# S5 octet steps of a hybrid decoder block at later places in the program: products and maps, the first states, all outputs

## The chip, the core and the metric

The kernel runs on one core of a Trainium2 chip. The metric is device time in microseconds, the median of the timed executions: 818.08 us for the kernel before (three runs, 817.52 to 818.77). The profile is that of one more execution, which took 814.82 us.

## The reference

One layer of a decoder trunk, width 2048, 512 tokens, batch 1. A normalised input goes through one wide projection, whose columns feed three head groups: an S5 branch (a diagonal complex state space model), differential attention, and cross-attention into 256 memory tokens. What they give is gated, put side by side, projected once more, normalised and added to the input.

```python
h = rmsnorm(x, g_pre)
cols = h @ w_in        # S5 u | S5 gate | diff q, k, v, gate | mem q, gate
...
# S5 branch: 64 groups of 16 channels, 64 complex states each
bu = einsum('tgh,gph->tgp', u, bbar)            # bbar, abar from dt, a, b
x_t = abar * x_{t-1} + bu_t                     # scan over the 512 tokens
y = Re(einsum('tgp,ghp->tgh', x, c)) + d * u    # then GELU, GLU, SiLU gate
...
out = x + rmsnorm(concat(heads) @ w_out, g_post)
```

## The kernel before

**The stream of chunks.** Every big matrix product is a list of chunks; one chunk is a piece of a weight matrix of 128x1024 values (512 KB). The chunks are worked off one after the other in the loop at the end of the kernel (from `for n, (_, f) in enumerate(chunks)`). For each, SyncE issues a DMA into `raw` (two buffers); ScalarE casts it to `whi` (three buffers), which holds the high part of the values; VectorE subtracts to get `wlo`, the rest; TensorE then does 24 matmuls of 128x512 in groups of three (`mm3`: high by high, low by high, high by low). The names `hhi`, `hlo` are the two parts of the normalised input. A load is issued two or three chunks ahead of its use, a cast one or two.

**The slots.** Each chunk is cut into four units of six matmuls. After each unit the loop calls what `at_slot(n, f)` has entered for that quarter of chunk n; `round(4 * n) + 3` is the number of the unit. So the table of slots (lines 716 to 744) says between which units a step stands in the program. TensorE keeps the program's order (`pin`). On VectorE, ScalarE and SyncE the scheduler that lays out the program orders the instructions, and each engine works its row off in that order.

**Stages.** Chunks 0 to 15 make u, the input of the S5 branch (eight column blocks of two chunks). Chunks 16 to 23 and 24 to 31 make the keys and values of the memory (the first of these with matmuls of 256 columns on `mhi`, `mlo`, the two parts of the memory tokens; a small step of TensorE on `diag`, the tokens' scales, stands soon after octet 3's weights). From chunk SG = 32 on come the S5 gate and further columns; from S1 = 64 on the GLU of the S5 branch.

**The S5 steps.** The 64 groups are handled as eight octets. For each octet there are, early:

- products (line 540), in two halves: VectorE makes `bp` and the first part of `dp` in the first half, `pm` and the rest of `dp` in the second. A DMA fetches `bc`, another writes `dp` to `sp_dr` in DRAM.
- maps (line 566): four transposes of `bp` by TensorE, a copy by ScalarE, a DMA to `sp_dr`.
- weights (line 573): 16 small matmuls of `dp` and `bp` by TensorE, then copies into `kz` and a DMA to `k_dr`.

And late, from chunk 33 on, one octet per 3.25 chunks:

- load (line 606): a DMA brings `sp_dr` back as `sp` (two buffers), the last reader of which is the octet's outputs.
- angles (line 632): GpSimd and VectorE make `cs`, ScalarE turns it into sine and cosine (three ACTIVATE rows on `cs`).
- spread (line 646): ScalarE copies `sp` into the two tiles `ub` (four copies).
- states (line 652), in six parts: 16 matmuls of `us` and `ub` by TensorE into two banks of `ps_s`; then VectorE's work: products with `cs` (`ra`), sums (`wre`, `wim`), eight scans (`zre`, `zim`), products again, and four writes to `x` (two per half).
- outputs (line 689): eight matmuls of `us` and `tm` and 16 of `x` and `sp` by TensorE into `ps_t`; then a GELU by ScalarE (square, tanh) and VectorE (`sq`, `ysb`); after each second octet DMAs to `y_dr`. `ge_open` reads it back for the GLU.

VectorE besides has `ut` and `ev` (evacuations of a finished column block), `mlo` (the low part of the memory tokens) and `wlo`. ScalarE has one table of functions at a time: between tanh and sine stands an ACT_TABLE_LOAD.

Lines 71, 96 and 99 of the profile are helpers: 71 is the line through which most instructions of the other engines are recorded, 96 a matmul, 99 a transpose. So groups and rows are told apart by the names of their tiles.

Of the kernel before, what the change touches and what calls it, by code (L numbers as in the profile page):

```python
# [54 lines left out]
def tile_hybrid_block(ctx: ExitStack, tc: tile.TileContext, a: dict, out: bass.AP):  # L55
# [33 lines left out]
    def psum(tag):  # L89
        return ps.tile([P, 512], F32, tag=tag, name=f"ps_{tag}", bufs={"mm": 4, "s": 2, "t": 2}[tag])  # L90
# [4 lines left out]
    def mm(*args, **kw):  # L95
        pin(pe.matmul(*args, **kw))  # L96
# [98 lines left out]
    def at_slot(n, f):  # L195
        side.setdefault(round(4 * n) + 3, []).append(f)
# [343 lines left out]
    def s5_products(o):  # L540


        bc = pt("bc", [512], 2)
        sy.dma_start(bc, a["bc"][o])
        gr = slice(8 * o, 8 * o + 8)

        def powers(t_, n):
            return t_[:, gr, :].unsqueeze(3).to_broadcast([P, 8, n, 16])

        def params(i, n):  # L550
            return bc[:, i * P:(i + 1) * P].rearrange("p (g h) -> p g h", g=8).unsqueeze(2).to_broadcast([P, 8, n, 16])

        bp, dp = pre["bp", o], pre["dp", o] = pt("bp", [8, LCH, 16]), pt("dp", [8, LCH + 1, 16], 2)
        m2 = pt("pm", [8, LCH + 1, 16])
        v.tensor_tensor(bp, powers(w1, LCH), params(0, LCH), ALU.mult)
        v.tensor_tensor(m2[:, :, 0:LCH], powers(w2, LCH), params(1, LCH), ALU.mult)
        v.tensor_tensor(bp, bp, m2[:, :, 0:LCH], ALU.add)
        v.tensor_tensor(dp, powers(pwr, LCH + 1), params(2, LCH + 1), ALU.mult)
        yield
        m2 = pt("pm", [8, LCH + 1, 16])  # L560
        v.tensor_tensor(m2, powers(npwi, LCH + 1), params(3, LCH + 1), ALU.mult)
        v.tensor_tensor(dp, dp, m2, ALU.add)
        sy.dma_start(sp_dr[o][:, 0:640], dp.rearrange("p g j h -> p (g j h)"))
        yield

    def s5_maps(o):
        pp_, up = psum("t"), pt("up", [512])
        for q in range(4):
            transpose(pp_[:, q * P:(q + 1) * P], pre["bp", o][:, 2 * q:2 * q + 2].rearrange("p x b h -> p (x b h)"))
        s.copy(up, pp_)  # L570
        sy.dma_start(sp_dr[o][:, 640:1152], up)
# [29 lines left out]
    oct_ = [{} for _ in range(8)]  # L601

    def t512(tag, bufs=1, shape=(P, 512)):
        return s5["wk"].tile(list(shape), F32, tag=tag, name=tag, bufs=bufs)

    def s5_load(o):

        sp = t512("sp", 2, (P, 1152))
        sy.dma_start(sp, sp_dr[o])
        oct_[o].update(dp=sp[:, 0:640].rearrange("p (g j h) -> p g j h", g=8, h=16), up=sp[:, 640:1152])  # L610
# [13 lines left out]
    def s5_toeplitz(i, x):  # L624

        tm = s5["d"][i % 2]["tm"]
        kd = k_dr[i].rearrange("(x q r) e -> x r q e", x=2, r=32)
        for b_ in range(LCH):
            r0 = 64 * x + 16 * b_
            sy.dma_start(tm[r0:r0 + 16, :, x * 64:(x + 1) * 64], kd[x, 0:16, :, 16 * b_:16 * b_ + 64])  # L630
# [15 lines left out]
    def s5_spread(o):  # L646
        for i in range(2):
            for x in range(2):
                rows = slice(64 * x, 64 * x + 64)
                s.copy(s5["ub"][i][rows, :, x], oct_[o]["up"][rows].rearrange("p (q i m) -> p q i m", q=4, i=2)[:, :, i])  # L650

    def s5_states(o):

        x, ub, us, (c_, s_) = s5["d"][o % 2]["x"], s5["ub"], oct_[o]["us"], oct_[o]["cs"]
        vre, vim = psum("s"), psum("s")
        for q in range(4):
            sl = slice(q * P, (q + 1) * P)
            mm(vre[:, sl], ub[0][:, q].rearrange("p x m -> p (x m)"), us[:, q], start=True, stop=True)
            mm(vim[:, sl], ub[1][:, q].rearrange("p x m -> p (x m)"), us[:, q], start=True, stop=True)
        yield  # L660
        a1, a2, a3, a4 = t512("ra", 2), t512("ra", 2), t512("ra", 2), t512("ra", 2)
        wre, wim = t512("wre"), t512("wim")
        v.tensor_tensor(a1, vre, c_, ALU.mult)
        v.tensor_tensor(a2, vim, s_, ALU.mult)
        v.tensor_tensor(wre, a1, a2, ALU.add)
        yield
        v.tensor_tensor(a3, vim, c_, ALU.mult)
        v.tensor_tensor(a4, vre, s_, ALU.mult)
        v.tensor_tensor(wim, a3, a4, ALU.subtract)
        yield  # L670
        zre, zim = t512("zre"), t512("zim")
        for q in range(4):
            sl = slice(q * P, (q + 1) * P)
            rbc = rch[:, 4 * o + q:4 * o + q + 1].to_broadcast([P, P])
            v.tensor_tensor_scan(zre[:, sl], rbc, wre[:, sl], 0.0, ALU.mult, ALU.add)
            v.tensor_tensor_scan(zim[:, sl], rbc, wim[:, sl], 0.0, ALU.mult, ALU.add)
        yield
        xg = x.rearrange("p (q x) c -> p q x c", x=2)
        for i, (y1, y2, op) in enumerate(((zre, zim, ALU.subtract), (zim, zre, ALU.add))):
            b1, b2 = t512("ra", 2), t512("ra", 2)  # L680
            v.tensor_tensor(b1, y1, c_, ALU.mult)
            v.tensor_tensor(b2, y2, s_, ALU.mult)
            for g_ in range(2):
                rows = slice(64 * g_, 64 * g_ + 64)
                b1_, b2_ = (t_[rows].rearrange("p (q c) -> p q c", q=4) for t_ in (b1, b2))
                v.tensor_tensor(xg[64 * i:64 * i + 64, :, g_, 1:], b1_, b2_, op)
            yield

    def s5_outputs(o):

        d, us = s5["d"][o % 2], oct_[o]["us"]
        yp = psum("t")
        cols_ = [slice(q * P, (q + 1) * P) for q in range(4)]
        for q in range(4):
            mm(yp[:, cols_[q]], s5["d"][o // 2 % 2]["tm"][:, 4 * (o % 2) + q], us[:, q], start=q == 0, stop=False,
               skip_group_check=True)
        for q in range(4):
            for x in range(2):
                mm(yp[64 * x:64 * x + 64, cols_[q]], oct_[o]["dp"][:, 2 * q + x, 1:].rearrange("p j h -> p (j h)"),
                   d["x"][:, 2 * q + x, 0:NCH], start=False, stop=True, tile_position=(0, 64 * x), skip_group_check=True)  # L700
        if o % 2 == 0:
            s5["y"] = t512("ysb", 2, (P, 2, 512))
        ysb = s5["y"]
        sq = t512("sq")
        s.activation(sq, yp, AF.Square)
        v.scalar_tensor_tensor(sq, sq, 1.0 / GELU_A, yp, ALU.add, ALU.mult)
        s.activation(sq, sq, AF.Tanh, scale=GELU_A * GELU_S)
        v.scalar_tensor_tensor(ysb[:, o % 2], sq, 1.0, yp, ALU.add, ALU.mult)
        if o % 2 == 1:
            dst = y_dr[o // 2].rearrange("(q x h) (j c) -> j x h q c", x=2, h=16, j=LCH)  # L710
            for x in range(2):
                for j in range(LCH):
                    r0 = 64 * x + 16 * j
                    sy.dma_start(dst[j, x], ysb[r0:r0 + 16].rearrange("p o (q c) -> p (o q) c", c=NCH))

    SG = S0 + 16
    STEPS = (0, 0.25, 0.75, 1, 1.5, 2)
# [1 line left out]
    at_slot(8, pre_open)  # L719
    at_slot(8, discretise)  # L720
    for o in range(8):
        e = 8.75 + 1.75 * o if o < 4 else 17.5 + 3.25 * (o - 4)
        d = 2 if o < 4 else 4
        at_slot(e, lambda o=o: (oct_[o].setdefault("pr", s5_products(o)), next(oct_[o]["pr"])))
        at_slot(e + d / 2, lambda o=o: next(oct_[o]["pr"]))
        at_slot(e + 0.75 * d, lambda o=o: s5_maps(o))
        at_slot(e + (2 if o < 4 else 3), lambda o=o: s5_weights(o))
# [3 lines left out]
    for o in range(8):  # L731
        e = SG + 1 + 3.25 * o
        at_slot(e - 0.75, lambda o=o: s5_angles(o))
        at_slot(e - 0.5, lambda o=o: s5_spread(o))
        for i in range(6):
            at_slot(e + STEPS[i] + (0 if o else 0.25), lambda o=o, i=i: (oct_[o].setdefault("st", s5_states(o)), next(oct_[o]["st"])))
        if o > 1:
            at_slot(e - 3, lambda o=o: s5_load(o))
            if o % 2 == 0:
                for x in range(2):  # L740
                    at_slot(e - 3.25 + 0.75 * x, lambda o=o, x=x: s5_u(o // 2, x))
                    at_slot(e - 4.5 + 0.75 * x, lambda o=o, x=x: s5_toeplitz(o // 2, x))
        at_slot(e + 3.25, lambda o=o: s5_outputs(o))
    S5_END = SG + 1 + 3.25 * 7 + 4.5


# [123 lines left out]
    for h in range(4):  # L870
        e = S2 + 2 + 3 * h
# [99 lines left out]
    for h in range(4):  # L971
        add_cols(a["w_in_a"], [20 + h], h_cols, NK, lambda i, acc, h=h: evac_k(h, acc))
        add_cols(a["w_in_a"], [16 + h], h_cols, NK, lambda i, acc, h=h: evac_q(h, acc))
        for qt in range(NT):
            e = S3 + 5 + 4 * h + (qt if h < 3 else qt // 2)
# [222 lines left out]
```

## Time and profile before

| | |
|---|---|
| timed runs, median | 818.08 us (817.52 to 818.77) |
| the profiled execution | 814.82 us |
| its span | 813.0 us |
| GpSimd (POOL) busy | 27.7 us |
| HBM traffic | 161 GB/s over the span |

A row of the timeline gives start, duration, engine, line, operation, tiles and count; in brackets stands how long the engine was idle before it and what ended that. A row of the table of waits gives the tile that the waiting instruction writes, the engine and tile waited for, then microseconds in all, how many times, and the longest. Matmul durations overlap their successors, so the pace is read from starts.

### The profile page before, as it was taken

How to read it: one execution, taken by the hardware profiler on the slowest of the kernel's cores; microseconds unless marked ns; L12 is line 12 of the kernel's file. 1: busy time of each engine (PE TensorE's matmuls, PEld its weight loads, DVE VectorE, ACT ScalarE, POOL GpSimd, SP SyncE). 2: the span in 40 equal slices, each digit the busy share in tenths (PEclk: the TensorE clock that was granted, in tenths of full speed). 3: DMA queues.
4: the chain of work that ended last, by engine and by line, in shares of the span. 5: the costliest groups of instructions: out<-in, count | busy, mean ns of one | idle time of the engine just before them, and what ended most of it. 6: DMA issues, size and time to landing. Idle time of an engine off the chain costs nothing.

```text
span 813.0 us, 10918 instructions
## 1 busy us (share of the span) xinstructions
PE 792.1 (97%) x4030; PEld 661.2 (81%) x4030; DVE 545.2 (67%) x1033; ACT 357.8 (44%) x593; POOL 27.7 (3%) x42
## 2 busy tenths in 40 slices
PE   8998999999999899999999999999999999999996
PEld 7876798778888787888888888888888888888885
DVE  4599978578887898847875544668888833132335
ACT  5654433433546344334733533446667532132311
POOL 0000000200000000000000000000100110000000
PEclk9999999999999999999999999999999999999999
DMA  7977767766445464367565222232224345322327
GB/s 262 369 271 248 259 218 250 251 176 190 134 151 174 112 165 116 120 171 260 185 209 168 93 92 91 78 104 78 79 77 145 96 155 174 104 86 96 114 95 258
DMA packets 60358, 131.59 MB, mean 162 GB/s; under 512 B 12689, under 2 KB 26129, under 8 KB 59409
## 3 DMA queue, kind: packets, MB, share of 16 engines
q1 hardware_dynamic: 60304, 130.91, 49.8%
q8 instruction: 31, 0.51, 0.3%
q14 instruction: 23, 0.18, 0.1%
HBM read 109.52 MB, written 21.36 MB: 161 GB/s over the span
## 4 chain that ended last, share of the span: by engine, by line
PE 73%; DVE 13%; DMA 5%; ACT 4%; issue 4%; SPq 1%; DVEq 0%; POOLq 0%; POOL 0%; ACTq 0%
PE ps_mm L96 65%; PE ps_s L96 4%; DVE wlo L71 3%; DVE ra L71 3%; DMA raw<-in_w_in_a_dram 2%; PE ps_t L96 2%; ACT whi L71 2%; PE ps_t L99 1%; DVE x L71 1%; DMA raw<-in_w_kv_b_dram 1%; ACT cs L71 1%; DMA sp<-sp_dr 1%; SPq L71 1%; DVE zim L71 1%; ACT L71 1%
## 5 line engine op out<-in xcount | busy, mean ns | idle before, releaser
L71 DVE TENSOR_TENSOR wlo<-raw,whi 128x1024 fp32r<-128x1024 f32 (+1 forms) x135 | 161.7, 1199 | 155.4 <-ACT whi L71 154.4
L71 ACT CAST whi<-raw 128x1024 fp32r<-128x1024 f32 (+1 forms) x135 | 138.7, 1029 | 258.4 <-PE ps_mm L96 144.0
L96 PE MATMUL ps_mm<-hhi,whi 128*128 128x512 f32 x512 | 201.5, 394 | 1.1 <-DVE ut L71 0.7
L96 PE MATMUL ps_mm<-hlo,whi 128*128 128x512 f32 x512 | 199.9, 390 | 0.7 <-DVE hlo L71 0.7
L96 PE MATMUL ps_mm<-hhi,wlo 128*128 128x512 f32 x512 | 199.6, 390 | 0.0
L96 PEld LDWEIGHTS ps_mm<-hhi,whi 128*128 128x128 f32 x512 | 96.2, 188 | 21.6 <-DVE ut L71 1.1
L96 PEld LDWEIGHTS ps_mm<-hhi,wlo 128*128 128x128 f32 x512 | 96.1, 188 | 20.6
L96 PEld LDWEIGHTS ps_mm<-hlo,whi 128*128 128x128 f32 x512 | 96.2, 188 | 20.5 <-DVE hlo L71 1.6
L96 PE MATMUL ps_mm<-whi,hhi 128*128 128x512 f32 x128 | 50.0, 390 | 0.0
L96 PE MATMUL ps_mm<-whi,hlo 128*128 128x512 f32 x128 | 49.9, 390 | 0.0
L96 PE MATMUL ps_mm<-wlo,hhi 128*128 128x512 f32 x128 | 49.9, 389 | 0.0
L96 PE MATMUL ps_mm<-whi,yshi 128*128 128x512 f32 (+1 forms) x112 | 43.9, 392 | 0.0
L96 PE MATMUL ps_mm<-wlo,yshi 128*128 128x512 f32 (+1 forms) x112 | 43.3, 387 | 0.0
L96 PE MATMUL ps_mm<-whi,yslo 128*128 128x512 f32 (+1 forms) x112 | 43.3, 386 | 0.0
L96 PEld LDWEIGHTS ps_mm<-whi,hlo 128*128 128x128 f32 x128 | 24.0, 188 | 5.1
L96 PEld LDWEIGHTS ps_mm<-wlo,hhi 128*128 128x128 f32 x128 | 24.0, 188 | 4.8
L96 PEld LDWEIGHTS ps_mm<-whi,hhi 128*128 128x128 f32 x128 | 24.0, 188 | 4.7
L71 DVE TENSOR_TENSOR x<-ra 64x512 f32<-64x512 f32 x32 | 26.3, 821 | 0.8
L71 ACT ACTIVATE pr<-sm,nm 128x128 f32<-128x128 f32 (+3 forms) x32 | 18.0, 564 | 18.9 <-DVE nm L71 18.6
L96 PE MATMUL ps_mm<-gehi,whi 128*128 128x512 f32 x64 | 25.2, 394 | 0.0
L96 PE MATMUL ps_mm<-gehi,wlo 128*128 128x512 f32 x64 | 25.1, 392 | 0.0
L96 PE MATMUL ps_mm<-whi,yxhi 128*128 128x512 f32 (+1 forms) x64 | 24.9, 389 | 0.0
(323 smaller groups left out, 1381.6 us busy)
## 6 DMA issues: line engine op xcount, KB each, us to landing
raw<-in_w_in_a_dram SPq DMA_DIRECT2D x63, 512.0 KB, 4.0
raw<-in_w_out_b_dram SPq DMA_DIRECT2D x32, 512.0 KB, 3.2
raw<-in_w_in_b_dram SPq DMA_DIRECT2D x16, 512.0 KB, 3.3
sp<-sp_dr SPq DMA_DIRECT2D x8, 576.0 KB, 4.5
rows<-in_x_dram SPq DMA_DIRECT2D x4, 1024.0 KB, 7.7
raw<-in_w_kv_a_dram SPq DMA_DIRECT2D x8, 512.0 KB, 3.6
raw<-in_w_kv_b_dram SPq DMA_DIRECT2D x8, 512.0 KB, 4.0
raw<-in_w_glu_a_dram SPq DMA_DIRECT2D x8, 512.0 KB, 5.1
```

What stands on the lines that cost most here:

```text
L71: r = f(*args, **kw)
L96: pin(pe.matmul(*args, **kw))
L99: pin(pe.transpose(o, i, ident))
```

## The change

Four numbers in the table of slots change. Products (both halves), maps and weights of octets 0 to 3 move by 0.75 chunk: from slots 8.75, 10.5, 12.25, 14 to 9.5, 11.25, 13, 14.75; those of octets 4 to 7 stay. The six parts of the states of octet 0 move by 0.25 chunk. The outputs of every octet move by 0.5 chunk, and with them the load of `sp` for octets 2 to 7. Slots that are not named stay, S5_END too. No instruction of the steps themselves is added or removed.

```diff
     for o in range(8):
-        e = 8.75 + 1.75 * o if o < 4 else 17.5 + 3.25 * (o - 4)
+        e = 9.5 + 1.75 * o if o < 4 else 17.5 + 3.25 * (o - 4)
         d = 2 if o < 4 else 4
...
         for i in range(6):
-            at_slot(e + STEPS[i] + (0 if o else 0.25), lambda o=o, i=i: (oct_[o].setdefault("st", s5_states(o)), next(oct_[o]["st"])))
+            at_slot(e + STEPS[i] + (0 if o else 0.5), lambda o=o, i=i: (oct_[o].setdefault("st", s5_states(o)), next(oct_[o]["st"])))
         if o > 1:
-            at_slot(e - 3, lambda o=o: s5_load(o))
+            at_slot(e - 2.5, lambda o=o: s5_load(o))
...
-        at_slot(e + 3.25, lambda o=o: s5_outputs(o))
+        at_slot(e + 3.75, lambda o=o: s5_outputs(o))
     S5_END = SG + 1 + 3.25 * 7 + 4.5
```

On VectorE, where the products of octet 0 are (after the first three `mlo` of a block of memory tokens), the row of before reads:

```order
L71 TENSOR_TENSOR bp<-w_155,bc 128x512
L71 TENSOR_TENSOR pm<-w_156,bc 128x8x64
L71 TENSOR_TENSOR dp<-pwr,bc 128x640
L71 TENSOR_TENSOR bp<-bp,pm 128x512
L71 TENSOR_TENSOR ut<-ps_mm,rb 128x512
L71 TENSOR_TENSOR wlo<-raw,whi 128x1024
L71 TENSOR_TENSOR pm<-npwi,bc 128x640
L71 TENSOR_SCALAR r_87<-rcol 128x4
L71 TENSOR_SCALAR r_88<-rcol 128x4
L71 TENSOR_TENSOR dp<-dp,pm 128x640
L71 TENSOR_TENSOR wlo<-raw,whi 128x1024
L71 SCALAR_TENSOR_TENSOR mlo<-mT,cols,mhi 128x256 x4
```

and that of the change, at the same place, from the `wlo` on:

```order
L71 TENSOR_TENSOR wlo<-raw,whi 128x1024
L71 TENSOR_TENSOR bp<-w_155,bc 128x512
L71 TENSOR_TENSOR pm<-w_156,bc 128x8x64
L71 TENSOR_TENSOR dp<-pwr,bc 128x640
L71 TENSOR_TENSOR bp<-bp,pm 128x512
L71 TENSOR_SCALAR r_87<-rcol 128x4
L71 TENSOR_SCALAR r_88<-rcol 128x4
L71 TENSOR_TENSOR wlo<-raw,whi 128x1024
L71 SCALAR_TENSOR_TENSOR mlo<-mT,cols,mhi 128x256 x4
L71 TENSOR_TENSOR pm<-npwi,bc 128x640
L71 TENSOR_TENSOR ut<-ps_mm,rb 128x512
L71 TENSOR_TENSOR dp<-dp,pm 128x640
```

An `ut` and a `wlo` now stand ahead of the first half (the `ut` one row above those shown), and a `wlo`, four `mlo` and an `ut` between the halves.

On TensorE, at the end of octet 0's share of the program, the row of before has the outputs of octet 0 right ahead of the states of octet 1:

```order
L96 MATMUL ps_mm<-hlo,whi 128x512
L96 MATMUL ps_mm<-hhi,wlo 128x512
L96 MATMUL ps_t<-us,tm_1696 128x128 x4
L96 MATMUL ps_t<-x_1697,sp 64x128 x8
L96 MATMUL ps_s<-us,ub_1694 128x128
L96 MATMUL ps_s<-us,ub_1695 128x128
```

With the change, the end of the two units that follow the states of octet 1 reads:

```order
L96 MATMUL ps_mm<-hhi,whi 128x512
L96 MATMUL ps_mm<-hlo,whi 128x512
L96 MATMUL ps_mm<-hhi,wlo 128x512
L96 MATMUL ps_t<-us,tm_1696 128x128 x4
L96 MATMUL ps_t<-x_1697,sp 64x128 x8
```

The states of octet 1 stand where they stood, and the outputs of octet 0 come twelve matmuls behind them, among the chunk's own. The same holds for each later octet.

On ScalarE, before, the copies `ub` of octet 3 (the two tiles are `ub_1694` and `ub_1695`) stand ahead of its sine steps on `cs`:

```order
L71 COPY ub_1694<-sp 64x4x64 x2
L71 COPY ub_1695<-sp 64x4x64 x2
L71 ACT_TABLE_LOAD
L71 ACTIVATE cs<-cs 128x512
L71 ACTIVATE sq<-ps_t 128x512
L71 ACTIVATE cs<-cs 128x512
L71 ACTIVATE cs<-cs,halfpi 128x512
```

With the change the same octet reads:

```order
L71 COPY ub_1694<-sp 64x4x64 x2
L71 ACT_TABLE_LOAD
L71 ACTIVATE cs<-cs 128x512
L71 COPY ub_1695<-sp 64x4x64
L71 ACTIVATE cs<-cs 128x512
L71 COPY ub_1695<-sp 64x4x64
L71 ACTIVATE cs<-cs,halfpi 128x512
```

Two of the four copies moved behind sine steps. In the next octet the order went the other way: before, it has table load, `cs`, table load, `sq`, `cs`, table load, `cs`; with the change, one table load, all three `cs`, the square, one table load, the tanh. In the last octet the four copies moved from behind the three `cs` and a cast to ahead of them.

## The prediction

> **What bounds the kernel now.** First the page's head and its table of busy times, then the table of what TensorE waited for.
>
> ```profile
> span 813.0 us, 10918 instructions
> PE 792.1 (97%) x4030; PEld 661.2 (81%) x4030; DVE 545.2 (67%) x1033; ACT 357.8 (44%) x593; POOL 27.7 (3%) x42
> PE ps_t L96 <- DVE x L71: 3.0, 2, 2.7
> PE ps_t L99 <- DVE bp L71: 2.7, 1, 2.7
> PE ps_s L96 <- ACT ub L71: 2.2, 3, 1.2
> PE ps_t L96 <- DVE dp L71: 1.4, 2, 1.0
> PE ps_t L96 <- DVE diag L71: 0.9, 1, 0.9
> ```
>
> TensorE is busy for 97% of the span, and the change neither adds nor removes a matmul. All that it can win is time in which TensorE stands still: the rows name 3.0 us for x (the outputs of an octet), 2.7 for bp (maps), 2.2 for ub (states), 1.4 for dp (weights), 0.9 for diag. The change moves the matmuls that wait; so the whole sum is these waits, before and after. The clock and VectorE's load come from the table of windows, for one octet of the S5 part, and the pace of the matmuls from two rows six matmuls (one unit) apart.
>
> ```profile
> 282.00:303.60 21.60, 21.60 (x119) 18.23 (x119) 19.71 (x32) 11.16 (x17) 1.09 (x1) 1.00 0.69 169
> 83.02 0.39 PE L96 MATMUL ps_mm<-hhi,wlo 128*128 128x512 f32 x1
> 84.38 0.39 PE L96 MATMUL ps_mm<-hhi,wlo 128*128 128x512 f32 x1
> ```
>
> The first row gives the stretch, the busy time and count of TensorE, its weight loads, VectorE, ScalarE and GpSimd, then TensorE's granted clock, the DMA share and GB/s. The clock is 1.00, so TensorE isn't throttled there. A matmul of 512 columns costs (84.38 − 83.02)/6 = 0.227 us, a unit 1.36. VectorE has 19.71 us of work in an octet's 21.6; its margin is 1.9. Both numbers come back below.
>
> **Edit 1: products, maps and weights of octets 0 to 3, three units later.** Maps and weights get 18 matmuls (4.08 us) more ahead of them; the products move in VectorE's queue. The timeline where the first octet's are:
>
> ```profile
> 70.43 0.39 PE L96 MATMUL ps_mm<-hhi,wlo 128*128 128x512 f32 x1
> 70.80 0.68 DVE L71 TENSOR_TENSOR bp<-w,bc 128x512 f32<-128x512 f32 x1
> 72.00 0.81 DVE L71 TENSOR_TENSOR dp<-pwr,bc 128x640 f32<-128x640 f32 x1
> 72.74 0.68 DVE L71 TENSOR_TENSOR bp<-bp,pm 128x512 f32<-128x512 f32 x1
> 73.34 1.06 DVE L71 TENSOR_TENSOR ut<-ps_mm,rb 128x512 f32<-128x512 f32 x1
> 73.47 0.66 PE L99 MATMUL ps_t<-cst,bp 128*128 128x128 f32 x4 [2.65 <-DVE bp L71]
> 74.32 1.22 DVE L71 TENSOR_TENSOR wlo<-raw,whi 128x1024 fp32r<-128x1024 f32 x1
> 75.46 0.82 DVE L71 TENSOR_TENSOR pm<-npwi,bc 128x640 f32<-128x640 f32 x1
> 76.33 0.82 DVE L71 TENSOR_TENSOR dp<-dp,pm 128x640 f32<-128x640 f32 x1
> 77.07 1.22 DVE L71 TENSOR_TENSOR wlo<-raw,whi 128x1024 fp32r<-128x1024 f32 x1
> 77.30 0.43 PE L96 MATMUL ps_t<-dp,bp 128*32 128x64 f32 x16 [0.42 <-DVE dp L71]
> 78.20 1.67 DVE L71 SCALAR_TENSOR_TENSOR mlo<-mT,cols,mhi 128x256 fp32r<-128x256 f32 x4
> ```
>
> Before: from the last matmul to the maps 73.47 − 70.43 − 0.23 = 2.81 us are lost, 0.16 more than the idle time shown (the restart); I add those 0.16 to every wait that goes or comes. At the weights that is 0.42 + 0.16 = 0.58. Together 3.39.
>
> After: VectorE is free at 70.80 and its new order is ut, wlo, bp, pm, dp, bp. By the starts above, ut costs 0.98, wlo 1.14, bp and pm 0.60, dp 0.74: 70.80 + 0.98 + 1.14 + 0.60 + 0.60 + 0.74 + 0.68 = 75.54. TensorE, which now has 18 matmuls more, arrives at 70.66 + 4.08 = 74.74, so **the maps wait 0.8 instead of 2.8**. Behind bp come the two r (0.1), wlo 1.14, four mlo 1.59 (1.67 less one overlap), pm 0.74, ut 0.98 and then dp 0.82: dp is done at 80.9. TensorE reaches the weights 0.42 + twelve matmuls (2.72) after the maps begin at 75.6, at about 78.8. **The weights wait 2.1 instead of 0.6**: the late second half of the products now stands behind a cast's subtraction, four mlo and an evacuation. Place: 2.9 for 3.39, or −0.5. Octets 1 to 3 do not wait now: the table has one wait for bp, and of the two for dp the longer belongs to octet 7, which isn't moved. Octets 1 and 2 I leave at none. Octet 3's weights now stand among the shorter matmuls of the next stage (256 columns), where TensorE comes sooner: between 0 and the 2.1 of octet 0 I take 0.6, nearer to the none of now. The diag step behind them (0.93) gets part of that time for its own input; I take 0.45 of it off. Edit 1 in all: **−0.4**; bounds −3.4 (no wait left) and +1.0 (the mlo of the next chunk also slip ahead of dp). The added DMA issues (bc, sp_dr, k_dr) move with their steps, and the first reader of sp_dr is some 80 us later: nothing.
>
> **Edit 2: states of octet 0 one unit later.**
>
> ```profile
> 167.12 1.26 ACT L71 COPY ub<-sp 64x256 f32<-64x256 f32 x3 [4.42 <-DMA sp<-sp_dr]
> 168.93 0.40 ACT L71 COPY ub<-sp 64x256 f32<-64x256 f32 x1
> 169.55 2.02 PE L96 MATMUL ps_s<-us,ub 128*128 128x128 f32 x16 [1.16 <-ACT ub L71]
> ```
>
> TensorE was ready 1.16 + 0.16 = 1.32 earlier, and now does six matmuls (1.36) first. ub is bound to the DMA that landed at 167.1, which does not move with TensorE. **−1.3**; bounds −1.32 and 0 (if the load slips by as much).
>
> **Edit 3: outputs of every octet two units later**, and the loads of sp half a chunk later with them. The states of the next octet now go first; then twelve matmuls; then the outputs. The outputs read x (VectorE). The only long wait:
>
> ```profile
> 260.87 0.69 DVE L71 SCALAR_TENSOR_TENSOR ysb<-sq,ps_t 128x512 f32<-128x512 f32 x1 [2.66 <-ACT sq L71]
> 261.38 1.28 ACT L71 ACT_TABLE_LOAD   x1
> 262.67 0.72 ACT L71 ACTIVATE cs<-cs,halfpi 128x512 f32<-128x512 f32 x1
> 263.43 1.29 DVE L71 TENSOR_TENSOR ra<-ps_s,cs 128x512 f32<-128x512 f32 x2 [1.87 <-ACT cs L71]
> 277.07 2.13 DVE L71 TENSOR_TENSOR x<-ra 64x512 f32<-64x512 f32 x2
> 278.54 0.43 PE L96 MATMUL ps_t<-x,sp 128*64 128x128 f32 x2 [2.69 <-DVE x L71]
> ```
>
> In octet 4 VectorE idled 2.66 and 1.87 us behind ScalarE, which mixed tanh and sine and so loaded its table three times; x was 2.69 late. In the new order ScalarE does all three cs steps, then both sq: two loads. And TensorE asks for x later by the 16 state matmuls (2.0) and twelve others (2.72), 4.7 in all, against 2.69 + 0.29 needed (the page's 3.0). The wait goes, though VectorE now takes its sq and ysb later. In the last octet ub stood behind three cs steps and a cast on ScalarE:
>
> ```profile
> 320.69 1.30 ACT L71 ACTIVATE cs<-cs 128x512 f32<-128x512 f32 x2 [6.22 <-DVE cs L71]
> 323.59 1.66 ACT L71 COPY ub<-sp 64x256 f32<-64x256 f32 x4
> 324.45 0.49 PE L96 MATMUL ps_s<-us,ub 128*128 128x128 f32 x2 [0.71 <-ACT ub L71]
> ```
>
> In the new order ub is ahead of cs, and the rest of the 2.2 us of ub (2.2 − 1.16 = 1.0, two waits) goes. Gain: 3.0 + 1.0 idle + four restarts of 0.16 = **−4.7**; bounds −4.7 and −2.4 (half of it given back to the later sq and ysb).
>
> What is late next: octet 3, where the new order on ScalarE puts two of the four ub behind sine steps (cs, ub, cs, ub).
>
> ```profile
> 215.27 0.69 DVE L71 SCALAR_TENSOR_TENSOR ysb<-sq,ps_t 128x512 f32<-128x512 f32 x1 [1.86 <-ACT sq L71]
> 230.42 1.65 ACT L71 COPY ub<-sp 64x256 f32<-64x256 f32 x4
> 230.98 1.05 PE L96 MATMUL ps_t<-us,tm 128*128 128x128 f32 x8
> 231.56 0.69 DVE L71 SCALAR_TENSOR_TENSOR cs<-cs 128x512 f32<-128x512 f32 x1
> ```
>
> One octet before 230.98, at 209.4 − 1.7 (edits 1 and 2) = 207.7, TensorE starts the states of octet 2; 2.0 + 2.7 later the outputs of octet 1, which end at 214.4. ScalarE's square, VectorE's sq, a table load and the tanh (0.6 + 0.7 + 1.3 + 0.6) bring ysb to 217.7 and its end to 218.3. In the trace the second cs step ends 16.3 after ysb; four ra, wre and a wlo (4.2) now stand ahead of ysb, and x (2.15) behind cs, so 9.95 remain: cs at 228.3. ScalarE's cs, ub, cs, ub (0.6 + 0.4 + 0.6 + 0.4) end at 230.3. TensorE asks at 230.98 − 1.7 + 0.1 = 229.4. Wait 0.9, with its restart **+1.1**; bounds 0 and +2.5.
>
> The Trainium skill, *ScalarE: Activation LUTs*, "What ACT_TABLE_LOAD costs", speaks against this part: a switch of tables is said to cost 1.283 us of load and about 1.38 of drain. By it each ysb would come some 1.4 later and the octet's margin of 1.9 nearly go, which is the third rival's way. The trace has the 1.28 and no drain (261.38 + 1.28, then cs at 262.67), so the sum goes without.
>
> **After the S5 part** the GLU follows; its S5_END slot is unmoved, but the last outputs are 2.7 later.
>
> ```profile
> 371.16 1.23 DVE L71 TENSOR_TENSOR wlo<-raw,whi 128x1024 fp32r<-128x1024 f32 x1 [1.72 <-ACT whi L71]
> 374.56 0.39 PE L96 MATMUL ps_mm<-gehi,wlo 128*128 128x512 f32 x1
> ```
>
> That chunk's wlo is ready at 372.4 and first read at 374.56: 2.2 in hand, against 2.7 for a load pushed back on SP's queue by the whole delay. Only part of it reaches that queue: 0; bounds 0 and +1.
>
> **Sum:** −0.4 − 1.3 − 4.7 + 1.1 + 0 = **−5.3 us**. The profiled run took 814.82 us with its span of 813.0, so 1.8 lie around the span; the span becomes 807.7 and that run 809.5. The median of the timed runs is 818.08, 3.3 above the profiled one; the same 5.3 taken from it gives **812.8**.
>
> **Rivals.**
> 1. *All waits go.* 3.39 + 1.3 + 4.7 = 9.4, giving 808.7. For it: 4.08 and 4.7 us of delay exceed every wait. Against: VectorE's new order keeps dp late at octet 0. Chance 0.16.
> 2. *The waits are passed on.* Edit 1 at +1.0, octet 3 at +2.5, the outputs at −2.4, edit 2 at −1.3: −0.2, giving 817.9. For it: VectorE and ScalarE take their steps in a fixed order, and each later step stands in front of others. Against: the later outputs ask for x 4.7 later, for 3.0 of wait. Chance 0.15. That nothing is won, because the moved steps' inputs move with them, has the same time and is counted here.
> 3. *VectorE becomes the bound: slower.* In the new order sq and ysb stand between the ra of the next octet. If VectorE idles once for tanh (1.86, at 215.27) and once for cs (1.87, at 263.43) in each octet, 19.71 + 3.73 = 23.4 exceeds 21.6 by 1.8; over seven octets 12.8, less the 6.4 of edits 1 to 3: +6.4, giving 824.5. It decides where these idle times pass 1.9 per octet. Against: in the window from 282 VectorE idled 1.9 in all, so not both times, and an idle time in front of sq is anchored to TensorE and shrinks when VectorE is late. Chance 0.09.
>
> The Trainium skill, *Perfetto Trace Analysis*, "Tensor Engine Instruction (MATMUL, LD_WEIGHTS)", holds that ACT and DVE work strictly first in, first out; by it nothing passes a waiting sq, as rival 3 needs. The row at 215.27 agrees: 1.86 us idle with other work queued behind it. It gives no time of its own.
>
> **The numbers.** My forecast has 0.60: with its own bounds −8 to −2.5, 810.1 to 815.6. The range must reach rival 1 and most of rival 2: 808.0 to 818.0 leaves out rival 3 and the edges of both, some 0.18. A difference under 0.2% (1.6 us) is about what a measurement cannot tell from none. Faster by more: 0.60 + 0.16 + 0.02 of rival 2 = 0.78; within: 0.12; slower: 0.10, nearly all rival 3.
>
> **What would show it.** Right: in the table of TensorE's waits x is gone, bp is near 0.7, dp grows to about 3.5 (three waits), ub is one wait of about 0.9 near 229 us, and the span is near 807.7. Wrong at edit 1: dp under 1 (rival 1) or bp above 2 (rival 2). Wrong at edit 3: x still in the table, or windows of an octet longer than 21.6 us with VectorE above 21 (rival 3). A new row for whi, wlo or raw near 370 us would mean that the GLU's loads were hit.

## The result, and the profile after

| | before | changed |
|---|---|---|
| timed runs | 818.26 us (median of 8) | 813.7 us (median of 8; 811.41 to 815.97) |
| ratio | | 0.9938, 95% interval 0.9915 to 0.996 |
| span of the profiled execution | 813.0 us | 813.9 us |
| its mean granted clock | 0.998 | 0.994 |

By the ratio the timed runs are 0.62% faster, 5.1 us (3.3 to 7.0). The two medians lie 4.6 us apart; the ratio comes out larger because one run of before took 822.6 us. The two profiled executions don't show the gain: the one of the change is even 0.9 us longer. So the profile is read place by place. In a later session one execution of best3 and one of before took 1131 us at a clock of 0.655; they are left out of every figure, and best3, whose profile is of that execution, is read by its times and the order of its instructions alone.

The table of TensorE's waits after the change:

```profile
PE ps_t L96 <- DVE dp L71: 4.2, 2, 2.2
PE ps_mm L96 <- DVE ut L71: 1.5, 1, 1.5
...
PE ps_s L96 <- ACT ub L71: 1.3, 1, 1.3
...
PE ps_t L99 <- DVE bp L71: 0.7, 1, 0.7
PE ps_t L96 <- DVE diag L71: 0.6, 1, 0.6
PE ps_t L96 <- DVE rm L71: 0.6, 1, 0.6
```

The row for x (3.0 before) is gone, bp fell from 2.7 to 0.7, ub from three waits to one. dp grew from 1.4 to 4.2. The timeline at octet 0 shows how (rows between those shown are left out):

```profile
76.56 0.39 PE L96 MATMUL ps_mm<-hhi,wlo 128*128 128x512 f32 x1
76.95 0.68 DVE L71 TENSOR_TENSOR bp<-bp,pm 128x512 f32<-128x512 f32 x1
77.69 0.66 PE L99 MATMUL ps_t<-cst,bp 128*128 128x128 f32 x4 [0.74 <-DVE bp L71]
77.70 1.21 DVE L71 TENSOR_TENSOR wlo<-raw,whi 128x1024 fp32r<-128x1024 f32 x1
78.83 1.66 DVE L71 SCALAR_TENSOR_TENSOR mlo<-mT,cols,mhi 128x256 fp32r<-128x256 f32 x4
80.42 0.81 DVE L71 TENSOR_TENSOR pm<-npwi,bc 128x640 f32<-128x640 f32 x1
80.74 0.39 PE L96 MATMUL ps_mm<-hhi,wlo 128*128 128x512 f32 x1
82.14 0.81 DVE L71 TENSOR_TENSOR dp<-dp,pm 128x640 f32<-128x640 f32 x1
83.09 0.43 PE L96 MATMUL ps_t<-dp,bp 128*32 128x64 f32 x16 [1.97 <-DVE dp L71]
83.45 0.58 PE L96 MATMUL ps_mm<-hhi,whi 128*128 128x512 f32 x1
...
87.21 0.39 PE L96 MATMUL ps_mm<-hhi,whi 128*128 128x512 f32 x1
```

From the last matmul to the maps 77.69 − 76.56 − 0.23 = 0.90 us are lost (2.81 before), to the weights 83.09 − 80.74 − 0.23 = 2.12 (0.58 before). Behind the weights the reader sees something new in the last two rows: they are nine matmuls apart, 2.04 us at the pace of before, and it took 3.76. The table of windows has the clock there as its last column but two:

```profile
84.00:87.00 3.00, 3.00 (x9) 2.32 (x8) 2.91 (x7) 0.00 (x0) 0.00 (x0) 0.50 0.98 317
83.00:87.00 4.00, 3.91 (x25) 3.08 (x26) 3.91 (x7) 0.24 (x1) 0.00 (x0) 0.59 0.94 303
...
160.00:180.00 20.00, 20.00 (x93) 16.71 (x92) 7.50 (x10) 7.06 (x11) 4.86 (x8) 0.94 0.92 256
```

TensorE's granted clock was 0.50 of full speed from 84 to 87 us and 0.59 in the mean from 83 to 87, and there is a second such stretch from 159 us on. In the S5 part, the states of octet 0 and of octet 7, which no longer wait, the one new wait (states of octet 3) and the slack of x (VectorE's last write for octet 4, the outputs that read it, and those of the next octet):

```profile
175.81 1.95 PE L96 MATMUL ps_s<-us,ub 128*128 128x128 f32 x16
...
235.58 0.63 ACT L71 ACTIVATE cs<-cs 128x512 f32<-128x512 f32 x1 [0.74 <-DVE cs L71]
...
237.06 0.40 ACT L71 COPY ub<-sp 64x256 f32<-64x256 f32 x1
237.51 1.83 PE L96 MATMUL ps_s<-us,ub 128*128 128x128 f32 x14 [1.26 <-ACT ub L71]
...
277.25 2.14 DVE L71 TENSOR_TENSOR x<-ra 64x512 f32<-64x512 f32 x2
...
286.23 1.10 PE L96 MATMUL ps_t<-x,sp 128*64 128x128 f32 x16
307.87 1.10 PE L96 MATMUL ps_t<-x,sp 128*64 128x128 f32 x16
323.98 1.95 PE L96 MATMUL ps_s<-us,ub 128*128 128x128 f32 x16
```

x is ready 6.8 us before it is read. ub of octet 3 waits for the sine steps that now stand ahead of it. And the weights of octet 7, which the change doesn't move:

```profile
155.81 1.23 DVE L71 TENSOR_TENSOR wlo<-raw,whi 128x1024 fp32r<-128x1024 f32 x1 [1.89 <-ACT whi L71]
157.80 0.83 DVE L71 TENSOR_TENSOR dp<-dp,pm 128x640 f32<-128x640 f32 x1
158.77 0.65 PE L96 MATMUL ps_t<-dp,bp 128*32 128x64 f32 x16 [2.22 <-DVE dp L71]
```

It waited 1.02 before and 2.22 now, for a dp that stands on VectorE behind a wlo, which hangs on a weight load (the cast ahead of it began at 154.72, 0.10 after that load had landed). The change has not made this difference. Up to 168 us every engine's order in ub_first, a run of the next section, is that of the changed kernel, and up to 187 us that in outputs_only is that of before; the same weights waited there (ub_first's row first):

```profile
154.53 0.43 PE L96 MATMUL ps_t<-dp,bp 128*32 128x64 f32 x16 [0.70 <-DVE dp L71]
```

```profile
156.62 0.43 PE L96 MATMUL ps_t<-dp,bp 128*32 128x64 f32 x16 [1.96 <-DVE dp L71]
```

So this wait differs by 1 us and more between executions of one and the same order.

The 0.9 us between the two spans come apart so: moved places −5.0 (octet 0 −0.4, octet 3's weights and diag +0.4, states of octet 0 −1.3, x and the last ub −5.1, ub of octet 3 +1.4); weights of octet 7, which vary by themselves, +1.2; the two stretches at a low clock +3.2; and, ahead of any moved step, +1.3 in the first weight loads and +0.8 at a ut at 52 us. These make +1.5, 0.6 more than measured; that rest is not assigned.

### The profile page after: what moved, and what is told of

Same layout as the page of the kernel before. It is cut to its first block, busy times and chain, and to the rows that moved or that the text cites. A ratio compares the mean times of both kernels' runs of the same rounds, so it can differ in the third digit from the quotient of the medians.

```text
span 813.9 us, 10924 instructions
## 1 busy us (share of the span) xinstructions
PE 794.4 (98%) x4030; PEld 663.2 (81%) x4030; DVE 545.2 (67%) x1033; ACT 358.9 (44%) x593; POOL 28.3 (3%) x42
## 4 chain that ended last, share of the span: by engine, by line
PE 82%; DVE 8%; DMA 4%; ACT 2%; issue 2%; SPq 1%; POOL 0%; DVEq 0%; POOLq 0%; ACTq 0%
PE ps_mm L96 71%; PE ps_s L96 7%; PE ps_t L96 3%; DMA raw<-in_w_in_a_dram 2%; DVE wlo L71 2%; PE ps_t L99 1%; DVE ra L71 1%; SPq L71 1%; DMA rows<-in_x_dram 1%; DMA par<-in_par_dram 1%; ACT whi L71 1%; DVE sm L71 1%; DVE x L71 1%; ACT cs L71 1%; DVE cs L71 0%
```

## The experiments

Each is given against the kernel before, timed in the same session. Diffs are against the changed kernel where nothing else is said.

| run | ratio (95%) | us |
|---|---|---|
| products_only | 1.0014 (0.9998 to 1.003) | +1.1 |
| outputs_only | 0.9949 (0.9929 to 0.997) | −4.2 |
| no_products | 0.9944 (0.9925 to 0.9963) | −4.6 |
| mm_late | 0.9953 (0.9937 to 0.9969) | −3.8 |
| mm_late_diag | 0.9938 (0.9918 to 0.9958) | −5.1 |
| half2_early | 0.9955 (0.9937 to 0.9974) | −3.7 |
| ub_first | 0.9935 (0.9913 to 0.9957) | −5.3 |
| best1 | 0.9885 (0.9867 to 0.9904) | −9.4 |
| half2_raw3 | 0.9892 (0.9868 to 0.9917) | −8.8 |
| best2 | 0.9894 (0.987 to 0.9918) | −8.7 |
| no_products_raw3 | 0.9924 (0.99 to 0.9948) | −6.2 |
| best3 | 0.9843 (0.9819 to 0.9868) | −12.8 |

The last column is the ratio applied to about 817.5 us. Intervals are some 1.5 to 2 us wide to each side, so neighbours in the table are not told apart.

**The parts alone.** products_only has edit 1, against before:

```diff
-        e = 8.75 + 1.75 * o if o < 4 else 17.5 + 3.25 * (o - 4)
+        e = 9.5 + 1.75 * o if o < 4 else 17.5 + 3.25 * (o - 4)
```

> Edit 1 alone (products, maps and weights of octets 0 to 3, 0.75 chunk later). Theory A (the time is TensorE's waits, at full clock): the maps' wait shrinks from 2.65 to 0.7 idle, the weights' grows from 0.42 to 2.0; -0.4 us, so within 0.2% of before. Theory B (a wait of 2 us or more at times also halves the clock for some 4 us behind it, 1.8 us each, as in the profile of the changed kernel behind two waits of 1.97 and 2.22): one long wait takes the place of another, so the same time as by A, but the windows behind 80 us may show a clock under 1.00. Rival C (edit 1 is what wins): -3 to -5.

Measured +1.1 us, between −0.2 and +2.5: no gain. Its table of waits has bp at 0.8, and dp at 4.8 in three waits (2.0 of it at octet 0); the rows of dp, x and ub:

```profile
PE ps_t L96 <- DVE dp L71: 4.8, 3, 2.3
PE ps_t L96 <- DVE x L71: 4.6, 4, 2.7
PE ps_s L96 <- ACT ub L71: 2.9, 2, 2.5
```

One long wait took another's place, and the clock halved behind octet 0's weights, as B had it. The states of octet 0 also waited longer than before (2.5 against 1.16): their sp took 8.3 us from its issue at 164.59 to the first copy ub, before 6.1 (160.98 to 167.12).

outputs_only has edit 3, against before:

```diff
-            at_slot(e - 3, lambda o=o: s5_load(o))
+            at_slot(e - 2.5, lambda o=o: s5_load(o))
...
-        at_slot(e + 3.25, lambda o=o: s5_outputs(o))
+        at_slot(e + 3.75, lambda o=o: s5_outputs(o))
```

> Edit 3 alone (outputs of every octet 0.5 chunk later, loads of sp with them). Theory A: the waits for x (3.0 idle) and the last octet's for ub (1.0) go, one for ub of octet 3 comes (1.3): -3.3 us, -0.4%. Theory B: besides one wait over 2 us goes, at times another 1.8: -3.3 to -5.1. Rival C (edit 1 is what wins): within 1.6 us of before.

Measured −4.2: nearly the whole of the change. The row for x is gone. no_products has edits 2 and 3:

```diff
-        e = 9.5 + 1.75 * o if o < 4 else 17.5 + 3.25 * (o - 4)
+        e = 8.75 + 1.75 * o if o < 4 else 17.5 + 3.25 * (o - 4)
```

> Edits 2 and 3 without edit 1. Theory A: -3.3 and the 1.3 of the states of octet 0: -4.6 us, within 0.4 of the changed kernel; the maps' wait of 2.7 for bp is back. Theory B: the same, and the long wait at the maps may be followed by a stretch at half clock. Rival C (edit 1 is what wins): under 1.6 us faster than before.

Measured −4.6, as forecast, and no different from the changed kernel. Rival C is out: edit 1 is not what wins. What edit 2 adds to edit 3, 0.4 by the ratios, is below the noise of either; its wait is gone from the trace.

**Why octet 0 wins nothing.** mm_late leaves VectorE's products at their old slots and moves only TensorE's steps:

```diff
-        e = 9.5 + 1.75 * o if o < 4 else 17.5 + 3.25 * (o - 4)
+        e = 8.75 + 1.75 * o if o < 4 else 17.5 + 3.25 * (o - 4)
...
-        at_slot(e + 0.75 * d, lambda o=o: s5_maps(o))
-        at_slot(e + (2 if o < 4 else 3), lambda o=o: s5_weights(o))
+        at_slot(e + (2.25 if o < 4 else 3), lambda o=o: s5_maps(o))
+        at_slot(e + (2.75 if o < 4 else 3), lambda o=o: s5_weights(o))
...
-    bp = pt("bp", [8, LCH, 16])
+    bp = pt("bp", [8, LCH, 16], 2)
```

> Edits 2 and 3, and of edit 1 only TensorE's share: maps and weights of octets 0 to 3 0.75 chunk later, the products' VectorE work at its old slots (bp with two buffers). Theory A: VectorE's order at octet 0 is that of before, bp is done at 73.4 and dp at 77.2 while TensorE comes 4 us later than before: both waits go, -4.6 - 3.4 = -8.0 us. Theory B: the only wait over 2 us that can be left is that of octet 7's weights, so stretches at half clock go too: -8.0 to -11, and single times closer together. Rival D (VectorE passes the delay on to diag or to octet 3's weights whatever its order): no better than the changed kernel, about -5.

Measured −3.8, a plain miss for theory A. Both waits at octet 0 did go, and then this stood in its table:

```profile
PE ps_s L96 <- ACT ub L71: 4.3, 4, 1.9
PE ps_t L96 <- DVE diag L71: 2.8, 1, 2.8
```

TensorE came some 2 us sooner to the diag step and stood there 2.8 instead of 0.9 us, and a stretch at half clock followed. The 4.3 of ub hold one more: the states of octet 0 waited 1.90 although edit 2 is in this kernel, as their sp took 9.0 us from issue to copy. Rival D had the diag step. Two runs ask what diag hangs on. mm_late_diag is mm_late with

```diff
-    at_slot(19, lambda: row_broadcast(rmb, rm, 2, mp))
+    at_slot(22, lambda: row_broadcast(rmb, rm, 2, mp))
```

> The run mm_late with the diag step (the broadcast of the memory tokens' scales by TensorE) three chunks later, slot 22 instead of 19. In mm_late both waits at octet 0 went, 3.4 us, but the diag step then waited 2.8 instead of 0.9 and was followed by a stretch at half clock. Theory E (what octet 0 wins is handed to the diag step, because diag stands on VectorE behind a wlo, four products and another wlo, which hang on the weight stream): with diag out of the way the 3.4 stay, -8 to -9 us against before. Rival F (the weight stream itself is the bound between 103 and 155 us, and TensorE then waits for whi, wlo or the weights of octet 7 instead): -4 to -6, with a new wait row of 2 us or more before 160 us.

and half2_early has the second half of the products ahead of the four mlo:

```diff
-        at_slot(e + d / 2, lambda o=o: next(oct_[o]["pr"]))
+        at_slot(e + (0.25 if o < 4 else 2), lambda o=o: next(oct_[o]["pr"]))
```

> The changed kernel with the second half of the products of octets 0 to 3 at e + 0.25 instead of e + 1, so that pm and dp stand ahead of the four mlo in VectorE's order. Theory A (waits add up): the weights' wait of 2.0 goes, -2 us against the changed kernel, some -7 against before. Theory E: dp's wait goes and the diag step takes it, its wait grows from 0.6 to 2 or more; the same time as the changed kernel, -4.5 to -5.5.

mm_late_diag measured −5.1; the wait went on to the weights of octet 4, from 116 us on, where it was 3.1 us for dp. half2_early measured −3.7: dp's wait at octet 0 is gone, and diag has it:

```profile
PE ps_t L96 <- DVE diag L71: 3.3, 1, 3.3
```

E foretold the second and failed on the first (it promised −8 to −9); rival F, the weight stream, fits both. Its trail is in the rows of half2_early:

```profile
105.63 0.33 SPq L71 DMA_DIRECT2D raw<-in_w_kv_a_dram  x1
110.96 1.05 ACT L71 CAST whi<-raw 128x1024 fp32r<-128x1024 f32 x1 [3.23 <-DMA raw<-in_w_kv_a_dram]
112.05 1.23 DVE L71 TENSOR_TENSOR wlo<-raw,whi 128x1024 fp32r<-128x1024 f32 x1 [3.91 <-ACT whi L71]
116.86 0.48 DVE L71 TENSOR_SCALAR diag<-cst,rm 128x128 f32<-128x128 f32 x2
117.29 1.19 PE L96 MATMUL ps_t<-diag,ones 128*128 128x128 f32 x4 [3.28 <-DVE diag L71]
```

The load of chunk 20 is issued at 105.63, once chunk 18's wlo has freed one of the two raw buffers; 5.2 us of load, a cast and the subtraction follow. VectorE stands idle for 3.91 us ahead of it, with the diag step queued behind it and behind octet 4's first products. half2_raw3 tests it. VectorE's order stays; a third buffer serves four of the loads, so chunk 20 needn't wait for chunk 18:

```diff
-    def load(src, pieces=1, beside=()):
-        raw = wp.tile([P, 1024], F32, tag="raw", name="raw", bufs=2)
+    def load(src, pieces=1, beside=(), third=False):
+        if third:
+            raw = mp.tile([P, 1024], F32, tag="raw3", name="raw3", bufs=1)
+        else:
+            raw = wp.tile([P, 1024], F32, tag="raw", name="raw", bufs=2)
...
-            raws.append(load(chunks[len(raws)][0]))
+            raws.append(load(chunks[len(raws)][0], third=len(raws) in (17, 20, 23, 26)))
```

> half2_early with a third buffer for the weight loads of chunks 17, 20, 23 and 26, nothing else; VectorE's order at the diag step stays. In half2_early the diag step waited 3.3 us. Theory F2 (the stream of weights, two buffers that each go through issue, load, cast and subtraction in 7.3 us a pair, sets when VectorE gets to wlo of chunk 20 and so to diag): chunk 20's load starts 2 us or more earlier, and the diag wait falls from 3.3 to 1.5 or less; -1.5 to -2 us against half2_early, some -6 against before, and fewer half-clock stretches. Rival H (diag waits for its own products or for ScalarE, not the stream): the wait stays at about 3.

Measured −8.8, 5 us better than half2_early; the two were timed in different sessions, but their intervals lie apart. The rows that answer to those above:

```profile
97.50 0.33 SPq L71 DMA_DIRECT2D raw<-in_w_kv_a_dram  x1
109.32 1.23 DVE L71 TENSOR_TENSOR wlo<-raw,whi 128x1024 fp32r<-128x1024 f32 x1 [1.19 <-ACT whi L71]
114.14 0.47 DVE L71 TENSOR_SCALAR diag<-cst,rm 128x128 f32<-128x128 f32 x2
114.56 0.68 PE L96 MATMUL ps_t<-diag,ones 128*128 128x128 f32 x4 [0.57 <-DVE diag L71]
```

Chunk 20's load went out at 97.50 instead of 105.63, its wlo was ready 2.7 us sooner, and diag waited 0.57 instead of 3.28 us. The two profiles run within 0.1 us of each other from 54 us up to the diag step; behind it half2_raw3 is 3.1 us ahead, and 5.2 at 123 us, where a stretch at half clock ends in half2_early that half2_raw3 lacks. Rival H is out, and this is shown, not argued: between about 104 and 120 us the two raw buffers set when VectorE gets on, and what TensorE wins ahead of that place it waits out there. no_products_raw3 asks whether the buffer wins by itself; it is no_products with the same edit.

> Edits 2 and 3 without edit 1 (as no_products), with the third buffer for the weight loads of chunks 17, 20, 23 and 26. Theory F2 (the stream swallows what octet 0 wins, at the diag step): without edit 1 there is little to swallow, so the buffer alone wins only the diag wait of 0.8 to 0.9; the waits for bp (2.7) and dp (0.5) at octet 0 stay, some -5.5 against before, and 3 us slower than half2_raw3. Rival I (the third buffer wins by itself, elsewhere in the stream): about as fast as half2_raw3, -8 or more.

Measured −6.2, its wait for bp of 2.7 back: near the −5.5 of F2, not the −8 of rival I. The edit of edit 1's region is then worth 2.6 us with the buffer and about nothing without; the intervals of these two still touch, so the sign of it rests on the waits more than on the times.

**The states.** ub_first moves the copies ub:

```diff
-        at_slot(e - 0.5, lambda o=o: s5_spread(o))
+        at_slot(e - 1, lambda o=o: s5_spread(o))
```

> The changed kernel with the copies ub of every octet half a chunk earlier (slot e - 1 instead of e - 0.5), so that ScalarE's order has all four ahead of the sine steps in octet 3 too. Theory A: the wait for ub at octet 3 (1.3 idle, 1.4 lost) goes and nothing takes it, as TensorE has no other wait for 60 us before or 500 behind it: -1.4 against the changed kernel, -6 to -6.5 against before. Rival G (the octets hang on each other through VectorE): the wait shows up at the next octet's x or ub, no gain.

Measured −5.3, no better than the changed kernel. The wait at octet 3 is gone, but octet 2 now has one of 1.2. The row of the waits, and that of octet 3's states in the timeline, whose 16 matmuls start in one piece and wait for nothing:

```profile
PE ps_s L96 <- ACT ub L71: 1.6, 2, 1.2
```

```profile
232.54 1.95 PE L96 MATMUL ps_s<-us,ub 128*128 128x128 f32 x16
```

The copies ub stand there on ScalarE behind a cast that waits for its weight load, which stands behind the loads of us on SyncE's queue:

```profile
208.35 1.05 ACT L71 CAST whi<-raw 128x1024 fp32r<-128x1024 f32 x1 [8.51 <-DMA raw<-in_w_in_a_dram]
209.30 1.66 ACT L71 COPY ub<-sp 64x256 f32<-64x256 f32 x4
```

So G's outcome, though not by VectorE as G had it. Nor has the edit made this wait: half2_raw3 (1.89) and mm_late (0.72) have it at octet 2 without the edit.

**Taken together.** best1 is mm_late_diag with ub_first's edit, the weights of octets 4 to 7 and the states of octet 0 another 0.25 chunk later:

```diff
-        at_slot(e + (2.75 if o < 4 else 3), lambda o=o: s5_weights(o))
+        at_slot(e + (2.75 if o < 4 else 3.25), lambda o=o: s5_weights(o))
...
-            at_slot(e + STEPS[i] + (0 if o else 0.5), lambda o=o, i=i: (oct_[o].setdefault("st", s5_states(o)), next(oct_[o]["st"])))
+            at_slot(e + STEPS[i] + (0 if o else 0.75), lambda o=o, i=i: (oct_[o].setdefault("st", s5_states(o)), next(oct_[o]["st"])))
```

> mm_late_diag, with ub ahead of the sine steps as in ub_first, the weights of octets 4 to 7 0.25 chunk later and the states of octet 0 another 0.25 chunk later: every place at which TensorE waits behind 60 us is moved. Theory B (half-clock stretches come behind waits of 2 us or more): with no such wait left, every run has a clock of 0.997 or more, and the times lie within 2 us of one another. If E holds too: -11 to -13 us against before, about 806. Rival F: -6 to -8.

Measured −9.4, between E's and F's. One long wait is left, again behind the weight stream, dp of octet 4. best2 takes it out of the way:

```diff
-        at_slot(e + d / 2, lambda o=o: next(oct_[o]["pr"]))
+        at_slot(e + (1 if o == 4 else d / 2), lambda o=o: next(oct_[o]["pr"]))
```

> best1 with the second half of the products of octet 4 one chunk earlier, so that pm and dp stand ahead of the wlo of chunk 22 in VectorE's order. In best1 the weights of octet 4 waited 3.0 us for dp and a half-clock stretch followed. Theory E: that wait goes, -3 us against best1, some -12 against before. Theory F2 (the stream sets the pace there): TensorE waits for wlo or whi of chunks 22 to 24 instead, 1 to 3 us in the table of waits; -1 against best1 at most. Theory B: without a wait of 2 us the clock is 0.997 or more in every run, and the times lie within 2 us.

Measured −8.7, no gain. The two tables, best1's row first:

```profile
PE ps_t L96 <- DVE dp L71: 3.0, 1, 3.0
```

```profile
PE ps_t L96 <- DVE diag L71: 3.7, 1, 3.7
```

The wait moved to the diag step. F2 was right that nothing is won, though its wait came at diag and not at a whi or wlo. best3 goes the other way: half2_raw3 with ub_first's edit and the states of octet 0 at 0.75.

> half2_raw3 with ub ahead of the sine steps (as ub_first) and the states of octet 0 another 0.25 chunk later. What half2_raw3 still waits for behind 60 us is maps 0.9, diag 0.7, ub of octets 0, 2 and 3 (0.5, 2.6, 1.5): F2 and A: the first and last of these ub waits go, -2 against half2_raw3, some -10.5 against before, 807 to 808; if ub of octet 2 goes too, -13. Theory B: with at most one wait of 2 us, the clock is 0.997 or more in nearly every run. Rival G (octets hang on each other): no better than half2_raw3.

Its five runs took 803.66 to 806.67 us: −12.8 us, the fastest of all, 0.9843 against the changed kernel's 0.9938. They had a clock of 0.997 or 0.998, as B had it. That is more than the −10.5 of F2 and A, and near the −13 given for the case that octet 2's wait goes too. Its copies ub of octet 2 still stand behind the cast, so whether that wait went is open.

## Why the prediction was right

**The total.** 812.8 us was forecast for 818.08, −5.3; measured were 813.7, and −5.1 by the ratio, −4.6 by the medians. The moved places came out at −5.0 in the profile, so the mechanism holds: the gain is TensorE's waits, those of x above all. That the total lies so near is partly luck, as the last point below shows. Of the signs named ahead, x gone, bp at 0.7 and one wait for ub came. dp is 4.2 in two waits instead of 3.5 in three, and the longer of the two is octet 7's. The span of 807.7 did not come: the eight runs have 809.6 to 813.9.

**Edit 1.** The two waits at octet 0 were forecast as 0.8 and 2.1 us lost and came out as 0.90 and 2.12; octet 3's dp as 0.6 and came out as 0.7. (The table names rm for it, 0.6, which VectorE ended 0.08 later; dp itself ended 0.14 ahead of the matmuls, as at octet 0.) Diag gave back 0.36, not 0.45. So edit 1 is about 0 at these places instead of −0.4, and products_only shows no gain. What the working lacked was the reason: the diag step was taken as a wait of its own, with "I take 0.45 of it off". It is where the weight stream collects what was won before; the changed kernel had won little ahead of it, mm_late and half2_early more. Rival 1, all waits go, did not come true under three other orders either (mm_late, half2_early, mm_late_diag): with two buffers the wait only moved on.

**Edit 2.** Right: −1.3, and no wait at octet 0's states in the profile after. But "does not move" is too firm for the load of sp: it took 6.1 us to the copy in before, 6.8 in the change and 9.0 in mm_late, which waits 1.90 there with this edit in it. The three profiles without the edit wait 0.96 to 2.51.

**Edit 3.** Right in each part: x and the last octet's ub are gone (−5.1 for −4.7), x has 6.8 us in hand, the new wait at octet 3 lost 1.4 for 1.1 forecast. outputs_only alone has −4.2 for −3.6. Rival 3 did not happen: the outputs at 286.23 and 307.87 start 21.64 us apart, so an octet still takes 21.6. The window of one octet there:

```profile
286.60:308.20 21.60, 21.60 (x122) 18.21 (x120) 19.60 (x32) 11.40 (x15) 1.09 (x1) 1.00 0.51 151
```

VectorE has 19.60 us of work in it, for 19.71 before.

**After the S5 part.** Right at 0: no wait for whi, wlo or raw near 370 us.

**What was not in it.** The step "the same 5.3 taken from" the median. The profiled run of before lay 3.3 us under its median, and this was taken over unexplained. The time goes with the clock, and that execution had 0.998. In the sessions of the experiments 64 timed runs of before had 0.989 to 0.998, and a straight line through them has 0.62 us more for each 0.001 of clock less (correlation −0.80). At 0.998 that line stands at 815.0 us, near the 814.82 of the profiled run; the line through the changed kernel's eight runs (0.994 to 0.998) stands at 811.2. That is 3.7 apart, and 2.9 when both get one slope. So an estimate: of the 5.1, 3 to 4 are waits, and the rest goes with a mean clock of 0.9955 instead of 0.9936. The forecast's 5.3 of waits was then too high by 1 to 2 us, and a gain in clock that it didn't contain made up for it. The −5.0 of the one profile doesn't settle this, as single waits vary by 1 us between executions. The split is loose: the changed kernel has eight runs, timed in another session, and single kernels stray from the rule (mm_late_diag's fastest run, 809.52, had 0.995, its slowest, 814.02, 0.998).

## What to carry to other kernels

A wait that is removed ahead of a stretch in which another stream (here two load buffers) sets the pace is waited out in that stretch: look first for the next place downstream where the queue behind a wait hangs on that stream, and relieve it there (a third buffer for four loads took diag's wait from 3.3 to 0.6 us). Moving the reader later works where nothing else stands behind it, as for x. When a profile's own time lies well off the median of the runs, find out why before its sum is carried over. Before a change of 1 us in one wait is put down to an edit, look at a second profile with the same order up to there: octet 7's weights differed by 1.5 us between two such.

## What the runs showed of the hardware

A wait of TensorE of about 2 us can halve its clock for some 3.4 us. In the profiles of before, the change and the eleven runs whose profile is read, 20 waits of 1.9 us or more lie between 60 and 800 us; 12 of them went with such a stretch. All five of 2.8 us or more are among them, and in that part no stretch came without one. Ten of the stretches began within 1.1 us after the end of the wait and lasted 3.4 us; those of half2_early and best1 began 1.3 and 0.5 us ahead of its end and lasted 6.8. The shortest wait with one was 1.96 us (outputs_only, at 157 us); the 1.97 at 83 us of the change cost nine matmuls 1.7 us more. The 2.65 and 2.69 of before went without, and so did the 1.98 of ub_first at the same place as that 1.97, in the same order.

The mean clock of the timed runs fits: 0.9932 for products_only, whose profile has four such waits, 0.9936 for before with two, 0.9945 to 0.9967 for those with one or two, 0.9974 for best3. But the counts come from one profile each, and whether best3's runs are free of such waits no profile shows. That the waits bring the stretches is supported by this and by their order in time, not shown by a run that changes nothing else; what decides between a wait with and one without was not tried.

The Trainium skill, *TensorE: Matmul & The Clock Gate*, "HAM oscillation — how this bites in real kernels", puts the danger at idle gaps over about 3.4 us; the 1.96 us here are well below it, and the measurement decides. The same page of the Trainium skill, "What's actually happening", says that the window over which activity is judged runs free of the kernel; that would fit 12 in 20, but no run here can show it.
